# A hybrid attention block on one core: which preparation of weights is tied behind the last heads' work

## The chip, the core and the metric

The kernel runs on one core of a Trainium2 chip. The metric is the device time of one execution in microseconds. The core has five engines that matter here: TensorE (PE; its weight loads are listed apart as PEld), VectorE (DVE), ScalarE (ACT), GpSimd (POOL) and SyncE (SP, which only issues transfers). Each has a queue of its own and works through it in the order in which the program was built; engines meet only where one waits for another's semaphore.

## What is computed

A block of a decoder over 512 positions with 1024 channels, in float32. One normalised input is projected to queries, keys, values and a gate z for two branches of 8 heads each; one branch is attention with forget gates ("f"), the other block-sparse attention with rotary positions ("m"). Each branch's output is multiplied by silu(z), projected, weighted by a sigmoid gate, added, projected once more and added to the input.

```python
h = rms_norm(x, norm_g[layer])
fq, fk, fv, fz, mq, mk, mv, mz, ga, gb, fl = split_cols(h @ w_in[layer], IN_SPLITS)
...
y_fox = from_heads(fox_attention(q, k, v, log_f)) * jax.nn.silu(fz)
...
y_moba = from_heads(moba_attention(q, k, v)) * jax.nn.silu(mz)
merged = (jax.nn.sigmoid(ga + b_gate[layer, 0]) * (y_fox @ w_fox[layer])
          + jax.nn.sigmoid(gb + b_gate[layer, 1]) * (y_moba @ w_moba[layer]))
x = x + merged @ w_out[layer]
```

## The kernel before, in words

Every matrix product is made of three: each operand is split into a high half (rounded to the matmul's format) and a low half (what is left), and high x high, high x low and low x high are added in PSUM. For weights this split is the *preparation* of a chunk of 128 x 1024 elements: ScalarE writes the high half `wh_...` (`split`, L131, L134), VectorE subtracts it from the raw chunk and writes the low half `wl_...` (L136). Raw chunks come by transfers on SyncE's queue into four buffers `wr`; the high and the low halves have four buffers each (`wh`, `wl`). A raw buffer is free again when its low half has been written, a half's buffer when the last matmul has read it.

The work is written as a list of *units*, each a handful of matmuls with their eviction. `stream` (L192) appends the loads and preparations of a weight to two lists, `loads` and `preps`, in the order of L989: ..., mvb, wf0, wf1, wf2, wf3, GZ0, GA0, ... `pump(i)` (L179) traces what is due: preparations up to number i + 3, and a load as soon as the preparation that frees its buffer has been traced. `filler` (L1011) wraps each unit of a list so that `pump` is called just ahead of it; `ahead` (L1008) shifts the number by -2 for wf, by -1 for the first two units of a q, k or v weight.

Attention goes by four groups of four heads (`plan`, L1070). For each group `attn_group` (L509) returns pieces: Tr (transposes of a pair of heads, queries and keys to `QS`, `KH`, `KL`), Aa (scores `lg`, row maximum `negm` on VectorE, exponential `p` on ScalarE), Bb (transposes of `p` into `p_a`, `p_b`, `p_cc`, their split into `pth` on ScalarE and `ptl` on VectorE, the product `pv` with the values, and its eviction: `ysh` on ScalarE, then `yma` or `ymb` on VectorE; `pv` has one PSUM bank), Yp (a multiplication on GpSimd). Between the pieces `inter` (L1030) traces the group's units. Within the last heads (group "m", "b") these are the last two units of mvb and the eight units of wf0 to wf3: the projection of the f branch, 12 matmuls of 512 columns each (`unit_f`, L670: `pf`, L666 to L668, evicted by ScalarE into `f` at L680; `pf` has two banks). The order that is traced there is Aa(0), mvb, Yp of the group before, mvb, Aa(1), wf0, Tr(1), wf0, Bb(0), wf1, Aa(2), wf1, Bb(1), wf2, Yp(0), wf2, Aa(3), wf3, Bb(2), wf3, Bb(3).

Then the stage "gates" begins (L1103) with GZ0: the z gate of the m branch, computed by seven products of sums of blocks (`group`, L694), in the order 0, 2, 1, 3, 5, 4, 6. Product 0 uses the raw chunk mza as it is, product 2 the other chunk of mza; product 1 and later ones use differences with mzb that VectorE forms in place (L702). The matmuls are L741 (high x high), L743 (low x high) and L744 (high x low).

The program's order on each engine is made when the kernel is built: a planner goes through the traced instructions, takes what is ready first by its own estimate of the times, and among those the one traced first. Two things bind it: data, and a tie. `tc.issue_after(ins)` ties: what is traced in its block on the engine of `ins` is queued behind `ins` on that engine. It is an order in the queue and no wait. `last_on(engine)` (L1027) is the instruction traced last on an engine. In the kernel before, `filler` puts such a block on VectorE around `pump` for all units of wf:

```python
def go(i=first_prep[nm] + ahead(nm, n), u=u, late=nm[:2] == "wf"):
    if late:
        with tc.issue_after(last_on(mybir.EngineType.DVE)):
            pump(i)
    else:
        pump(i)
    u()
```

Of the kernel before, what the change touches and what calls it, by code (L numbers as in the profile page):

```python
# [29 lines left out]
def fox_moba_kernel(ctx: ExitStack, tc, xT, x, w_in, w_fl, w_fox, w_moba, w_out, cst, rope, out):  # L30
# [10 lines left out]
    stage = {}  # L41

    def enter(name):
        if stage:
            stage.pop("guard").__exit__(None, None, None)
        stage["guard"] = tc.tile_pool(name=name, bufs=1, reuse_waits="tile")
        stage["pool"] = stage["guard"].__enter__()
# [43 lines left out]
    def col(c, n=1):  # L91
        return cs[:, c:c + n]
# [3 lines left out]
    ones = con.tile([P, P], F32, name="ones")  # L96
    mask = con.tile([P, 512], F32, name="mask")
    enter("start")
    first_loads()
    wsc = t2("u", 3, "wsc", (P, 2))  # L100
# [75 lines left out]
    loads, preps, first_prep = [], [], {}  # L176
    done = {"loads": 0, "preps": 0}

    def pump(i):  # L179

        while True:
            j = done["loads"]
            if j < len(loads) and (j < WR or loads[j - WR][1] < done["preps"]):
                loads[j][0]()
                done["loads"] += 1
            elif done["preps"] < len(preps) and done["preps"] <= i + 3:
                preps[done["preps"]]()
                done["preps"] += 1
            else:
                return  # L190
# [65 lines left out]
    def make_sums(k):  # L256
        a, b = XT[k], XT[k + 4]
        out = []
        for o, x, y, op in ((b[:, HT:S], a[:, HT:S], b[:, HT:S], OP.add), (a[:, HT:S], a[:, 0:HT], a[:, HT:S], OP.subtract),
                            (a[:, 0:HT], b[:, HT:S], a[:, 0:HT], OP.subtract), (b[:, 0:HT], b[:, 0:HT], a[:, 0:HT], OP.subtract)):  # L260
            V.tensor_tensor(out=o, in0=x, in1=y, op=op)
        for i, f in enumerate((a, b)):
            hi = t2("sm", 2, "sum_h", dt=F32R)
            A.activation(hi, f, AF.Copy)
            V.tensor_tensor(out=f.bitcast(F32R), in0=f, in1=hi.bitcast(F32), op=OP.subtract)
            out.extend((d[2 * i:2 * i + 2, :, k, :].rearrange("s p t -> p s t"),
                        t.rearrange("p (s t) -> p s t", t=HT)) for d, t in zip(S_dram, (hi.bitcast(F32), f)))

        def store():
            for d, t in out:  # L270
                A.dma_start(out=d, in_=t)
        return store

    def load_sums():
        for i in (1, 0, 3, 2):
            SB[i] = [stage["pool"].tile([P, 4, HT], F32R, name=f"S{i}{hl}") for hl in "hl"]
            for d, t in zip(S_dram, SB[i]):
                nc.gpsimd.dma_start(out=t.bitcast(F32), in_=d[i])
# [65 lines left out]
    def rope_tables():  # L344
        nc.sync.dma_start(out=rp, in_=rope)
        for nm, c in (("mq", C_GQ), ("mk", C_GK)):
            tab = con.tile([P, NT, 32], F32, name=f"tab_{nm}")
            g = col(c, 16)
            G.tensor_tensor(out=tab[:, :, 0:16], in0=rp[:, :, 0:16],
                            in1=g[:, None, :].to_broadcast([P, NT, 16]), op=OP.mult)  # L350
            G.tensor_tensor(out=tab[:, :, 16:24], in0=rp[:, :, 16:24],
                            in1=g[:, None, 8:16].to_broadcast([P, NT, 8]), op=OP.mult)
            G.tensor_tensor(out=tab[:, :, 24:32], in0=rp[:, :, 24:32],
                            in1=g[:, None, 0:8].to_broadcast([P, NT, 8]), op=OP.mult)
            CA[nm] = tab
# [69 lines left out]
    def zero_kl():  # L425

        for o in range(2):
            Q2t[o] = stage["pool"].tile([P, S], F32R, name=f"Q2{o}")
        for b in range(2):
            for o in range(2):  # L430
                KLt.setdefault(o, []).append(stage["pool"].tile([P, S], F32R, name=f"KL{o}{b}"))
        for o in range(2):
            rows = slice(HD, P) if o == 0 else slice(0, HD)
            for tl in KLt[o] + [Q2t[o]]:
                G.memset(tl[rows, :].bitcast(F32), 0.0)
# [51 lines left out]
    def moba_begin():  # L487
        for o in range(2):
            rows = slice(HD, HD + 32) if o == 0 else slice(0, 32)
            for tl in KLt[o]:  # L490
                G.memset(tl[rows, :].bitcast(F32), 0.0)
# [503 lines left out]
    def units(name):  # L995
        k = name[:2]
        if k[0] == "G":
            return groups[name]
        if k == "wf":
            return [unit_f(int(name[2]), c) for c in range(2)]  # L1000
        if k == "wm":
            i = int(name[2])
            return [lambda c=c: merge_a(i, c) for c in range(2)]
        if k[1] == "z":
            return [unit_z(name, c) for c in range(2)]
        return [unit(name, t) for t in range(4)]

    def ahead(nm, n):  # L1008
        return n if nm[0] == "G" else -2 if nm[:2] == "wf" else -1 if nm[1] in "qkv" and n < 2 else 0

    def filler(names):  # L1011
        res = []
        for nm in names:
            nm, _, part = nm.partition(":")
            for n, u in enumerate(units(nm)):
                def go(i=first_prep[nm] + ahead(nm, n), u=u, late=nm[:2] == "wf"):
                    if late:
                        with tc.issue_after(last_on(mybir.EngineType.DVE)):
                            pump(i)
                    else:  # L1020
                        pump(i)
                    u()
                if not part or str(n) in part:
                    res.append(go)
        return res

    def last_on(engine):  # L1027
        return next(i for i in reversed(nc.cur_bb.bb.instructions) if i.engine == engine)

    def inter(a, b):  # L1030
        n, m = len(a), len(b)
        ia = ib = 0
        while ia < n or ib < m:
            if ib >= m or (ia < n and ia * m <= ib * n):
                a[ia]()
                ia += 1
            else:
                b[ib]()
                ib += 1

    def seq(names):
        for u in filler(names):
            u()
# [13 lines left out]
    forget_exp()  # L1057
    norm_row()
    pump(0)
    fz = filler(["fza", "fzb"])  # L1060
    for k, u in enumerate(fz):
# [3 lines left out]
    forget()  # L1065
    seq(["fva"])
    enter("attention")
    zero_kl()
    rope_tables()
    plan = (("f", "a", C_FQ, C_FK, ["fkb", "fqb", "fvb"]),  # L1070
# [5 lines left out]
    for n in range(4):  # L1076
        nxt = []

        def following(n=n, nxt=nxt):
            br, half, cq, ck = plan[n + 1][:4]  # L1080
            if n == 1:
                moba_begin()
            nxt.extend(attn_group(br, half, col(cq), col(ck)))
            nxt[0][0]()
        fill = filler(plan[n][4])
        if n < 2:
            for k, at in ((2 * n, 2), (2 * n + 1, 6)):
                store = []

                def with_sums(u=fill[at], k=k, store=store):  # L1090
                    u()
                    with tc.issue_after(last_on(mybir.EngineType.DVE)):
                        store.append(make_sums(k))

                def with_store(u=fill[at + 1], store=store):
                    u()
                    store[0]()
                fill[at], fill[at + 1] = with_sums, with_store
        inter(body + ([following] if n < 3 else []) + tail, fill)
        if n < 3:  # L1100
            body, tail = nxt[1][:1] + gate + nxt[1][1:], nxt[2]
            gate = nxt[3]
    enter("gates")  # L1103
    load_sums()
    for n, u in enumerate(filler(["GZ0"])):
# [135 lines left out]
```

## Time and profile before

| | |
|---|---|
| median of 3 runs | 424.71 us (424.6 to 425.9) |
| profiled execution | 424.55 us, span 422.8 us |
| TensorE matmul busy | 415.2 us, 98% of the span |
| TensorE weight loads busy | 387.7 us, 92% |
| VectorE busy | 334.5 us, 79% |
| ScalarE busy | 273.6 us, 65% |
| GpSimd busy | 109.5 us, 26% |
| granted TensorE clock | 0.998 of full speed |

The profile is of one execution; its time contains the span from the first to the last instruction and what lies around it. Busy shares are means over stages with different limits. The end of a matmul is modelled, so the timeline of TensorE is best read by its starts. In a timeline the columns are start and duration in us, engine, line, operation, the tile written and those read, partitions x elements, count; in brackets at the end the idle time of that engine just before and what ended it.

### The profile page before, as it was taken

What the parts mean: (1) busy time and instruction counts of PE and PEld (TensorE: products, weight loads), DVE (VectorE), ACT (ScalarE), POOL (GpSimd) and SP (SyncE); (2) the same over time, 40 slices, a digit from 0 to 9 for tenths busy, and PEclk for the clock granted to TensorE, in tenths of its full rate; (3) what the DMA queues carried; (4) which work ended last, traced back from release to release, by engine and by line L of the source; (5) the groups of instructions that cost most, each with busy time, mean ns of one, the idle gap of its engine ahead of it and who ended that gap; (6) DMA issues with size and microseconds to landing.
All of it is one profiled execution on the core that took longest, in us unless ns stands there. A gap on an engine that the chain in (4) does not pass through costs nothing.

```text
span 422.8 us, 7826 instructions
## 1 busy us (share of the span) xinstructions
PE 415.2 (98%) x2956; PEld 387.7 (92%) x2956; DVE 334.5 (79%) x571; ACT 273.6 (65%) x521; POOL 109.5 (26%) x127
## 2 busy tenths in 40 slices
PE   7999999999999999999999999999999999999996
PEld 6998899999999999999988789999999989988884
DVE  4669978798889877597457769998998675788982
ACT  4985337877788767797379845666756525685550
POOL 1059300252023880417501042134000020022240
PEclk9999999999999999999999999999999999999999
DMA  7981244654264432241211039705151726796494
GB/s 246 399 314 50 60 140 137 183 165 154 50 226 120 158 101 80 71 121 32 99 34 44 28 96 373 252 13 188 39 162 52 248 51 152 243 246 108 82 159 159
DMA packets 26373, 59.52 MB, mean 141 GB/s; under 512 B 3168, under 2 KB 7968, under 8 KB 26336
## 3 DMA queue, kind: packets, MB, share of 16 engines
q1 hardware_dynamic: 13552, 38.38, 27.5%
q0 software_dynamic: 3968, 9.44, 10.4%
q10 hardware_dynamic: 8816, 11.21, 9.1%
q8 instruction: 23, 0.38, 0.4%
q14 instruction: 14, 0.11, 0.1%
HBM read 48.37 MB, written 6.32 MB: 129 GB/s over the span
## 4 chain that ended last, share of the span: by engine, by line
PE 83%; DVE 6%; DMA 5%; ACT 2%; issue 2%; SPq 1%; DVEq 0%; ACTq 0%
PE pb_GB L744 3%; PE pb_GA L744 3%; PE pb_GA L741 3%; PE pb_GB L741 3%; PE pb_GA L743 3%; PE pb_GB L743 3%; PE po L943 3%; PE po L945 3%; PE po L944 3%; PE pv L609 2%; PE pv L610 2%; PE lg L556 2%; PE lg L555 2%; PE pf L666 2%; PE pf L668 2%; DMA x<-in_x_dram 2%
## 5 line engine op out<-in xcount | busy, mean ns | idle before, releaser
L330 POOL TENSOR_TENSOR ff<-ss,mh 128x8 f32<-128x8 f32 x16 | 28.3, 1771 | 59.4 <-DVE ss L328 58.8
L560 ACT ACTIVATE p<-p,negm 128x128 f32<-128x128 f32 (+1 forms) x64 | 35.6, 557 | 8.9 <-DVE negm L558 8.6
L558 DVE CUSTOM_DVE_ANT_0 p<-lg,mask 128x128 f32<-128x128 f32 (+1 forms) x64 | 30.2, 485 | 8.3 <-PE lg L556 6.9
L134 ACT ACTIVATE wh_GB<-wr_gb 128x1024 fp32r<-128x1024 f32 x14 | 14.6, 1058 | 13.9 <-PE pm L667 5.9
L905 ACT ACTIVATE wh_o<-wr_o 128x1024 fp32r<-128x1024 f32 x14 | 14.8, 1060 | 9.7 <-PE pb_GB L743 2.8
L555 PE MATMUL lg<-KH,QS 128*128 128x128 f32 (+1 forms) x64 | 20.9, 332 | 0.0
L136 DVE TENSOR_TENSOR wl_GB<-wr_gb,wh_GB 128x1024 fp32r<-128x1024 f32 x14 | 16.8, 1220 | 5.0 <-ACT wh_GB L134 5.0
L136 DVE TENSOR_TENSOR wl_GA<-wr_ga,wh_GA 128x1024 fp32r<-128x1024 f32 x14 | 19.2, 1388 | 1.5 <-ACT wh_GA L134 1.5
L906 DVE TENSOR_TENSOR wl_o<-wr_o,wh_o 128x1024 fp32r<-128x1024 f32 x14 | 16.9, 1220 | 2.4 <-ACT wh_o L905 2.3
L134 ACT ACTIVATE wh_GA<-wr_ga 128x1024 fp32r<-128x1024 f32 x14 | 14.4, 1056 | 6.9 <-DVE wr_ga L702 3.0
L826 POOL DMA_DIRECT2D uGB<-f x4 | 3.5, 871 | 58.2 <-issue 48.2
L529 DVE SCALAR_TENSOR_TENSOR QS<-p_qT,cs,QS 64x512 fp32r<-64x512 f32 x16 | 12.0, 750 | 5.7 <-ACT QS L528 5.4
L606 DVE TENSOR_TENSOR ptl<-p_b,pth 128x512 fp32r<-128x512 f32 x16 | 11.0, 684 | 6.2 <-ACT pth L605 6.1
L528 ACT ACTIVATE QS<-p_qT,cs 64x512 fp32r<-64x512 f32 x16 | 10.9, 681 | 4.4 <-PE p_qT L519 3.0
L744 PE MATMUL pb_GA<-Gh,wl_GA 128*128 128x256 f32 x48 | 13.5, 281 | 0.0
L744 PE MATMUL pb_GB<-Gh,wl_GB 128*128 128x256 f32 x48 | 13.5, 281 | 0.0
L743 PE MATMUL pb_GA<-Gl,wh_GA 128*128 128x256 f32 x48 | 13.5, 281 | 0.0
L741 PE MATMUL pb_GA<-Gh,wh_GA 128*128 128x256 f32 x48 | 13.5, 281 | 0.0
L741 PE MATMUL pb_GB<-Gh,wh_GB 128*128 128x256 f32 x48 | 13.5, 280 | 0.0
L743 PE MATMUL pb_GB<-Gl,wh_GB 128*128 128x256 f32 x48 | 13.5, 280 | 0.0
L666 PE MATMUL pf<-yhf,wh_wf 128*128 128x512 f32 x32 | 13.0, 407 | 0.3 <-ACT f L680 0.3
L668 PE MATMUL pf<-yhf,wl_wf 128*128 128x512 f32 x32 | 12.6, 403 | 0.2 <-DVE wl_wf L136 0.2
(483 smaller groups left out, 1821.4 us busy)
## 6 DMA issues: line engine op xcount, KB each, us to landing
wr_ga<-in_w_in_dram SPq DMA_DIRECT2D x8, 512.0 KB
wr_gb<-in_w_in_dram SPq DMA_DIRECT2D x8, 512.0 KB
wr_o<-in_w_out_dram SPq DMA_DIRECT2D x8, 512.0 KB
xt<-in_xT_dram SPq DMA_DIRECT2D x8, 256.0 KB
x<-in_x_dram SPq DMA_DIRECT2D x8, 256.0 KB
KH<-KH ACTq DMA_DIRECT2D x16, 128.0 KB
s_dramh<-sum_h ACTq DMA_DIRECT2D x8, 256.0 KB
s_draml<-xt ACTq DMA_DIRECT2D x8, 256.0 KB
```

The costliest lines, as they stand in the source:

```text
L134: A.activation(hi[:, :, 0:n], src, AF.Copy)
L136: eng.tensor_tensor(out=lo[:, q, 0:n], in0=src[:, q], in1=hi[:, q, 0:n].bitcast(F32), op=OP.subtract)
L330: G.tensor_tensor(out=f2, in0=ss.rearrange("p t h -> p (t h)"), in1=mh, op=OP.pow)
L555: T.matmul(lg[:, :n], qs[:, qt], kh[:, :n], start=True, stop=False)
L558: V.tensor_tensor_reduce(pt, lg[:, :n], mask[:, 512 - n:512], -0.125, 3.0e38, op0=OP.add, op1=OP.min, accum_out=mkn[:, hh, i:i + 1])
L560: A.activation(pt, pt, AF.Exp, bias=mkn[:, hh, i:i + 1], scale=-1.0, accum_out=rs[:, hh, i:i + 1])
L666: T.matmul(p, hi[:, k, cc], yh, start=(k == 0), stop=False)
L668: T.matmul(p, lo[:, k, cc], yh, start=False, stop=(k == 3))
L741: T.matmul(o, hi[:, k, cc], lh, start=(n < 3 and c == 0 and k == 0), stop=False, skip_group_check=True)
L743: T.matmul(o, hi[:, k, cc], ll, start=False, stop=False, skip_group_check=True)
L744: T.matmul(o, lo[:, k, cc], lh, start=False, stop=(k == 3), skip_group_check=True)
L906: V.tensor_tensor(out=wide(lo), in0=wide(R[key, c]), in1=wide(hi).bitcast(F32), op=OP.subtract)
```

## The change

The tie around `pump` for all wf units goes. In its place `pump` itself ties single preparations: those from z's first on (number `first_prep["GZ0"]` and above) that are traced while the heads are being traced, and those on two engines, behind the last VectorE and the last ScalarE instruction traced before them. A key "heads" in the dictionary `stage` says that the heads are being traced; `enter` therefore asks for the key "guard" instead of a dictionary that isn't empty.

```diff
     def enter(name):
-        if stage:
+        if "guard" in stage:
...
             elif done["preps"] < len(preps) and done["preps"] <= i + 3:
-                preps[done["preps"]]()
+                with ExitStack() as ties:
+                    if done["preps"] >= first_prep["GZ0"] and "heads" in stage:
+                        for engine in (mybir.EngineType.DVE, mybir.EngineType.Activation):
+                            ties.enter_context(tc.issue_after(last_on(engine)))
+                    preps[done["preps"]]()
                 done["preps"] += 1
...
-                def go(i=first_prep[nm] + ahead(nm, n), u=u, late=nm[:2] == "wf"):
-                    if late:
-                        with tc.issue_after(last_on(mybir.EngineType.DVE)):
-                            pump(i)
-                    else:
-                        pump(i)
+                def go(i=first_prep[nm] + ahead(nm, n), u=u):
+                    pump(i)
                     u()
...
     enter("attention")
+    stage["heads"] = True
...
+    stage.pop("heads")
     enter("gates")
```

## Rows read from the trace of the kernel before

**Rows 1.** Windows: window, its length, busy us (instructions) per engine, clock, DMA share, GB/s

```profile
core 0: us, PE busy (x) PEld busy (x) DVE busy (x) ACT busy (x) POOL busy (x), PEclk, DMA share, GB/s
210.00:220.00 10.00, 10.00 (x70) 9.29 (x70) 6.05 (x14) 7.57 (x15) 0.00 (x0) 1.00 0.13 29
220.00:230.00 10.00, 9.66 (x57) 8.08 (x56) 7.26 (x19) 8.49 (x21) 1.30 (x1) 1.00 0.15 40
230.00:240.00 10.00, 10.00 (x60) 8.33 (x59) 6.03 (x19) 8.76 (x23) 0.00 (x0) 1.00 0.10 26
240.00:250.00 10.00, 9.43 (x48) 7.36 (x48) 5.81 (x12) 6.00 (x17) 0.76 (x1) 1.00 0.21 68
250.00:260.00 10.00, 10.00 (x66) 8.93 (x65) 9.93 (x11) 4.45 (x7) 5.50 (x8) 1.00 0.86 272
300.00:320.00 20.00, 20.00 (x171) 20.00 (x170) 19.31 (x21) 12.96 (x19) 0.00 (x0) 1.00 0.34 107
```

**Rows 2.** Timeline of TensorE (PE) in the last heads

```profile
226.56 0.39 PE L555 MATMUL lg<-KH,QS 128*128 128x512 f32 x1
226.79 0.39 PE L556 MATMUL lg<-KL,QS 128*128 128x512 f32 x1
227.51 0.50 PE L666 MATMUL pf<-yhf,wh_wf 128*128 128x512 f32 x1 [0.34 <-ACT f L680]
...
233.67 0.60 PE L599 MATMUL p_b<-ident,p 128*128 128x128 f32 x4
234.02 0.48 PE L610 MATMUL pv<-ptl,v_mvb 128*128 128x512 f32 x1
...
240.01 0.63 PE L599 MATMUL p_a<-ident,p 128*128 128x128 f32 x4
240.99 0.50 PE L609 MATMUL pv<-pth,v_mvb 128*128 128x512 f32 x1 [0.35 <-DVE ymb L635]
...
241.56 0.34 PE L609 MATMUL pv<-pth,v_mvb 128*128 128x384 f32 x1
...
242.12 0.50 PE L668 MATMUL pf<-yhf,wl_wf 128*128 128x512 f32 x1 [0.22 <-DVE wl_wf L136]
...
249.97 0.60 PE L599 MATMUL p_a<-ident,p 128*128 128x128 f32 x4
250.47 0.50 PE L668 MATMUL pf<-yhf,wl_wf 128*128 128x512 f32 x1
...
256.12 0.37 PE L741 MATMUL pb_GZ<-Gh,wh_GZ 128*128 128x256 f32 x1
```

**Rows 3.** Timeline of VectorE (DVE) in the last heads

```profile
222.46 0.69 DVE L606 TENSOR_TENSOR ptl<-p_b,pth 128x512 fp32r<-128x512 f32 x1 [1.82 <-ACT pth L605]
...
240.25 0.68 DVE L635 TENSOR_TENSOR ymb<-pv,ysh 64x512 f32<-64x512 f32 x1
240.86 1.21 DVE L136 TENSOR_TENSOR wl_wf<-wr_wf,wh_wf 128x1024 fp32r<-128x1024 f32 x1
...
244.13 0.18 DVE L575 RECIPROCAL rinv<-rsum 128x8 f32<-128x8 f32 x1
248.47 0.70 DVE L635 TENSOR_TENSOR ymb<-pv,ysh 64x512 f32<-64x512 f32 x1 [4.16 <-ACT ysh L634]
249.20 1.23 DVE L136 TENSOR_TENSOR wl_wf<-wr_wf,wh_wf 128x1024 fp32r<-128x1024 f32 x1
250.34 2.31 DVE L136 TENSOR_TENSOR wl_GZ<-wr_mza,wh_GZ 128x1024 fp32r<-128x1024 f32 x1
```

**Rows 4.** Timeline of ScalarE (ACT) in the last heads

```profile
217.01 1.06 ACT L134 ACTIVATE wh_wf<-wr_wf 128x1024 fp32r<-128x1024 f32 x1
...
222.33 1.06 ACT L134 ACTIVATE wh_GZ<-wr_mza 128x1024 fp32r<-128x1024 f32 x1
...
226.86 0.60 ACT L680 ACTIVATE f<-pf 128x512 f32<-128x512 f32 x1
...
242.71 0.72 ACT L560 ACTIVATE p<-p,negm 128x512 f32<-128x512 f32 x1 [0.32 <-DVE negm L558]
```

**Rows 5.** Waits of SyncE's queue, 195 to 300 us: total, times, longest

```profile
SPq L707 <- DVE wl_wf L136: 61.3, 3, 39.6
```

## The prediction

> **What bounds the kernel now.** I first read the windows view over the stage in question [rows 1]. From 300 to 320 us TensorE is busy all the time and takes 171 matmuls of 256 columns in 20.00 us: that is how the back of the kernel looks, a TensorE that waits for nothing. In the last heads it is different: between 220 and 250 us TensorE shows 0.34 and 0.57 us of idle time, and VectorE and ScalarE, busy for 5.8 to 8.8 of 10 us, are not full either. So the bound there is the order of the queues, not an engine.
>
> Busy time hides part of it, because the end of a matmul is modelled. So the second view is TensorE's timeline [rows 2], read from start to start: undisturbed, 512 columns take 0.23 us to the next start (226.56 to 226.79), four transposes 0.35 (233.67 to 234.02), 384 columns some 0.17 (an estimate: three quarters of 0.23). What a start comes later than that is lost, and the first matmul behind a stall takes 0.50 instead of 0.39, another 0.10 (rounded down). There are four such places:
> - 226.79 to 227.51: 0.72 - 0.23 + 0.10 = 0.59, waiting for ScalarE's eviction f.
> - 240.01 to 240.99: 0.98 - 0.35 + 0.10 = 0.73, waiting for VectorE's ymb.
> - 241.56 to 242.12: 0.56 - 0.17 + 0.10 = 0.49, waiting for wl_wf.
> - 249.97 to 250.47: 0.50 - 0.35 + 0.10 = 0.25, where the row names no releaser, but the matmul reads the wl_wf that VectorE finished at 250.43 [rows 2, 3].
> The sum is 2.06 us, and the change can hardly give back more: behind these places TensorE's matmuls stand at full rate.
>
> The third and fourth views tell why [rows 3, 4]. VectorE issues the third and fourth low halves of wf at 240.86 and 249.20, each right behind ymb or with it just done (240.25; 248.47), which is the tie that the code draws. Yet their high halves were long there: the last ran on ScalarE at 217.01. And VectorE was idle meanwhile: 1.82 us ahead of 222.46, 4.16 us ahead of 248.47. On ScalarE z's first high half (wh_GZ) runs at 222.33, without a tie, 34 us before its first reader on TensorE at 256.12 [rows 2], and 4.5 us ahead of the eviction f at 226.86 for which TensorE then waits.
>
> **The change part by part.** The pump runs ahead of the units: mvb's units trace the preparation of wf0 and wf1, wf1's and wf2's units that of wf2 and wf3, wf3's that of z's first product. So the removed tie concerned three VectorE splits (wf2, wf3, z's first), and the new one concerns z's first alone, on both engines.
>
> 1. *wf2's and wf3's low halves lose their tie.* Two splits of 1.21 and 1.23 us [rows 3] can go as soon as their high halves are there, by 218.1 at the latest (217.01 + 1.06). Nothing is added or removed; they move ahead of head work by some 20 to 30 us. What they gain is the two waits: -0.49 and -0.25. What they cost is what they push back on VectorE: 2.44 us. Cover: between 210 and 220 VectorE is idle for 3.95 of 10 us [rows 1], and 1.82 us more before 222.46, and TensorE meanwhile has wf0's matmuls. I take the cost at nothing, since the idle time there (5.8 us at most) is over twice the work. If the cover fails, each split holds up the head's next small operation by up to 1.22, 2.44 in all; the other end is nothing.
>
> 2. *z's first high half gets a tie on ScalarE*, behind the last exponential traced, at 242.71 [rows 4]. It leaves 222.33 with its 1.06 us and comes at 243.4 at the earliest. ScalarE's queue between the two places moves up by at most 1.06; TensorE lost 0.59 to that queue. What stands between wh_GZ and f are head operations that wait for TensorE and VectorE themselves, so not all of it comes back: between 0 and -0.59, and I take the middle, -0.30. The second product's high half is traced behind the heads and has no tie, but takes the next of the same four wh buffers; I expect it behind the first, and count nothing for it.
>
> 3. *z's first low half keeps its place in the tracing order*, behind the reciprocal at 244.13, as before; today it ran at 250.34, since it stood behind wf3's split [rows 3]. After the change it may fill the 4.16 us in which VectorE waited for ScalarE's ysh. High half 243.4 to 244.5, low half to about 245.7: 10 us before 256.12. Cost nothing, the cover being those 10 us; were it gone, the price is the split itself, 1.22.
>
> 4. *SyncE's queue.* The loads of z's other two raw weights stand at its head and wait 61.3 us in all (three waits) for wl_wf, up to 39.6 us at once [rows 5]. With the splits early they go about 20 us earlier, 2 x 512 KB into a stretch in which the DMA engines are 0.10 to 0.15 busy [rows 1]; today they fall beside the loads of 250 to 260 (0.86). No TensorE row waits for them today: nothing. The heads' small transfers between 210 and 240 could meet them, which is one more way to part 1's price, not a further one.
>
> 5. *The wait at 240.99.* Its releaser is ymb, which the change does not touch; but wf2's matmuls no longer lack their low half and could stand in that hole. Between 0 and -0.73; I take 0, for the row that names the releaser.
>
> The sum: -0.49 - 0.25 - 0.30 = -1.04 us. The profiled execution took 424.55 us (span 422.8), 0.16 below the median of 424.71, so 423.51 for an execution like it and **423.7 us** for the median: 0.24% less. Whether this reaches the end: from 256 on TensorE is full, the preparation of z starts no later than before, and VectorE has 2.44 us less to do in the crowded 250 to 260 (9.93 of 10), so the later stages can move up as a whole.
>
> How much there is to win at all can also be read off the weight loads: PEld is idle 1.92 + 1.67 + 2.64 + 1.07 = 7.3 us between 220 and 260 [rows 1]. If all of that were waiting, the hole would be three times mine. The rows speak against it: a load takes 20.00 / 170 = 0.12 us in the full stretch, a matmul of 512 columns 0.23, so wf's matmuls leave the loader idle even undisturbed. The Trainium skill (Perfetto Trace Analysis, Identifying the Most-Contended Engine) says to judge TensorE's headroom by the busy share of LDWEIGHTS, not of matmuls; by that rule the change could win up to 7.3 us, by start-to-start 2.06.
>
> **The rivals.** What a measurement of this kernel can tell from no change is about 0.3%, 1.27 us: above 425.98 is slower, below 423.44 faster.
>
> *More comes back* (30%): with wf2 and wf3 free, the hole at 240 is filled too, and all of f's wait goes: -2.06, 422.65 us. For it: TensorE's order is planned with what is ready, and more is ready at every point. Against: an order fixed beforehand that met four holes will meet others.
>
> *It does not do what it says* (11%): the splits go early but TensorE's order stays, and the holes are waited out for pth, ymb or f instead; only the smallest, 0.25, goes: 424.46 us.
>
> *Slower* (16%): the untied splits get in front of head operations in VectorE's queue, which runs in order. Place: the chain score, maximum, exponential, pth, ptl of the last heads, where at 240.99 TensorE takes up ymb's result without any slack. Price: 2 x 1.22 in full, less what still comes back (0.74 + 0.30): +1.40, 426.1 us. It decides once a split stands closer than 1.22 us before an operation for which TensorE has no other work; against it speaks the idle time between 210 and 222.
>
> *The loader's whole idle time is waiting* (2%): 7.3 us come back, 417.4 us. The start-to-start readings speak against nearly all of it. The rule of the Trainium skill named above (Perfetto Trace Analysis) would allow this time at most.
>
> **How the numbers follow.** My forecast has the remaining 41%, of which some 4 points fall below 423.44 (f's wait gone in full gives 423.4). Faster: 30 + 2 + 4 = 0.36. Same: 37 + 11 = 0.48. Slower: 0.16. The range leaves out the slower case at its full price and the loader's, 18%; it reaches from 422.4 (422.65 and a quarter for the spread of the runs) to 425.8 (the median and most of one exposed split). The likeliest case alone: 423.4 to 424.4.
>
> **What would show it.** Right: wl_wf three and four before 225 on VectorE, no wait of TensorE for wl_wf, wh_GZ's first at 243 or later and no long run of ScalarE work from 222 to 227; wr_mzb loaded before 230; the first matmul of pb_GZ about 1 us earlier, and the same lead at 300 and at the end. Wrong: a new wait of TensorE for QS, negm, pth or ymb between 214 and 255 (slower), or pb_GZ's first matmul waiting for its weights; or a lead at 256 that is gone by 320, which would say that VectorE and not TensorE sets the pace there.

## The result and the profile after

The changed kernel takes 427.74 us (median of 8 runs, 427.05 to 428.2) against 425.22 us (424.6 to 427.0) before: a ratio of 1.0054 (95% interval 1.0038 to 1.007; intervals stand in square brackets from here on). That is 0.54% slower, above the 425.8 us at which the range ended. The profiled execution took 427.42 us with a span of 425.7 us, 2.9 us more than the 422.8 before.

Line numbers behind L188 are 4 higher than before (`pf` is L670 to L672, `ptl` L610, the products of GZ L745 to L748); the split keeps L134 and L136.

First the windows of the changed kernel; the first five rows answer to [rows 1].

```profile
core 0: us, PE busy (x) PEld busy (x) DVE busy (x) ACT busy (x) POOL busy (x), PEclk, DMA share, GB/s
220.00:230.00 10.00, 9.36 (x55) 7.71 (x54) 8.34 (x25) 8.01 (x22) 0.25 (x1) 1.00 0.31 98
230.00:240.00 10.00, 10.00 (x51) 8.34 (x51) 4.58 (x13) 5.87 (x16) 1.05 (x1) 1.00 0.08 16
240.00:250.00 10.00, 10.00 (x61) 8.82 (x60) 4.10 (x11) 6.83 (x17) 0.00 (x0) 1.00 0.08 25
250.00:260.00 10.00, 10.00 (x70) 9.19 (x69) 9.19 (x16) 7.02 (x15) 5.76 (x9) 1.00 0.57 208
260.00:270.00 10.00, 8.40 (x71) 8.20 (x70) 9.11 (x10) 6.63 (x8) 1.68 (x1) 1.00 0.76 274
270.00:280.00 10.00, 10.00 (x87) 10.00 (x86) 9.46 (x10) 5.38 (x8) 2.38 (x2) 1.00 0.51 177
280.00:290.00 10.00, 10.00 (x87) 10.00 (x86) 9.97 (x9) 6.08 (x8) 5.18 (x3) 1.00 0.14 46
290.00:300.00 10.00, 8.82 (x74) 8.61 (x74) 9.80 (x10) 6.24 (x8) 0.74 (x1) 1.00 0.48 166
```

The stage that was to gain has gained: TensorE shows no idle time from 230 to 260. The loss stands behind it, 1.60 us in 260 to 270 and 1.18 in 290 to 300, both stretches in which TensorE of the kernel before was full (10.00). VectorE does less than before in 230 to 250 (4.58 and 4.10 of 10 us for 6.03 and 5.81); from 250 to 300 it is over 9 of 10 busy in every stretch, as it was before (9.27 to 9.93).

TensorE's timeline, which answers to [rows 2], and below it the waits of TensorE from 195 to 320 us (total, times, longest):

```profile
227.59 0.39 PE L560 MATMUL lg<-KL,QS 128*128 128x512 f32 x1
228.56 0.50 PE L670 MATMUL pf<-yhf,wh_wf 128*128 128x512 f32 x1 [0.58 <-ACT f L684]
...
249.97 0.39 PE L560 MATMUL lg<-KL,QS 128*128 128x512 f32 x1
...
255.60 0.37 PE L745 MATMUL pb_GZ<-Gh,wh_GZ 128*128 128x256 f32 x1
...
265.80 0.28 PE L747 MATMUL pb_GZ<-S0l,wh_GZ 128*128 128x256 f32 x1
267.68 0.39 PE L748 MATMUL pb_GZ<-S0h,wl_GZ 128*128 128x256 f32 x1 [1.60 <-DVE wl_GZ L136]
...
290.41 0.28 PE L747 MATMUL pb_GA<-Gl,wh_GA 128*128 128x256 f32 x1
291.88 0.38 PE L748 MATMUL pb_GA<-Gh,wl_GA 128*128 128x256 f32 x1 [1.18 <-DVE wl_GA L136]
```

```profile
PE pb_GZ L748 <- DVE wl_GZ L136: 1.6, 1, 1.6
PE pb_GA L748 <- DVE wl_GA L136: 1.2, 1, 1.2
PE pf L670 <- ACT f L684: 0.6, 1, 0.6
```

No matmul waits for wl_wf or for ymb any more. Read from start to start as in the prediction, and summed over all starts from 220 to 260, TensorE lost 4.02 us before (1.19 + 0.85 + 1.63 + 0.35 by stretches of 10) and loses 2.96 now (1.72 + 0.22 + 0.62 + 0.40): 1.06 less. (The sums depend on what one takes as undisturbed for each shape, their difference hardly.) The first matmul of `pb_GZ` starts 0.52 earlier, at 255.60 for 256.12 [rows 2]; some 0.5 us had been lost before 195 us, where TensorE's matmuls stand in the same order in both kernels. Behind that the two new stalls cost about 1.82 and 1.46 us from start to start. 0.5 - 1.06 + 1.82 + 1.46 = 2.7 of the 2.9 us.

VectorE's timeline, which answers to [rows 3], with z's chain up to product 3 and the triple of low halves in front of the second stall:

```profile
215.42 1.23 DVE L136 TENSOR_TENSOR wl_wf<-wr_wf,wh_wf 128x1024 fp32r<-128x1024 f32 x1
...
219.04 1.23 DVE L136 TENSOR_TENSOR wl_wf<-wr_wf,wh_wf 128x1024 fp32r<-128x1024 f32 x1
...
252.93 0.20 DVE L579 RECIPROCAL rinv<-rsum 128x8 f32<-128x8 f32 x1
253.88 2.36 DVE L136 TENSOR_TENSOR wl_GZ<-wr_mza,wh_GZ 128x1024 fp32r<-128x1024 f32 x2 [0.74 <-ACT wh_GZ L134]
...
257.30 0.67 DVE L639 TENSOR_TENSOR ymb<-pv,ysh 64x512 f32<-64x512 f32 x1
257.90 0.67 DVE L610 TENSOR_TENSOR ptl<-p_a,pth 128x512 fp32r<-128x512 f32 x1
258.50 0.67 DVE L610 TENSOR_TENSOR ptl<-p_b,pth 128x512 fp32r<-128x512 f32 x1
259.09 1.21 DVE L706 TENSOR_TENSOR wr_mzb<-wr_mzb,wr_mzb 128x1024 f32<-128x1024 f32 x1
...
266.40 1.22 DVE L136 TENSOR_TENSOR wl_GZ<-wr_mzb,wh_GZ 128x1024 fp32r<-128x1024 f32 x1
...
286.13 5.69 DVE L136 TENSOR_TENSOR wl_GA<-wr_ga,wh_GA 128x1024 fp32r<-128x1024 f32 x3
```

The low half that ends the first stall (266.40 to 267.62) ran in the kernel before here:

```profile
262.83 1.22 DVE L136 TENSOR_TENSOR wl_GZ<-wr_mzb,wh_GZ 128x1024 fp32r<-128x1024 f32 x1
```

There it was done at 264.05, 2.5 us before it was wanted (266.56). It now comes 3.57 us later and is wanted 0.6 us earlier (265.92), so the slack is turned into a stall. Its chain begins with the pair at 253.88, for 250.34 [rows 3]: the same 3.5 us. From the pair to this low half VectorE takes 12.5 us in both kernels, with ptl and ymb of the last heads between z's instructions in both. The chain has not become longer; all of it starts later.

Why is z's pair late? ScalarE's timeline answers to [rows 4], SyncE's to [rows 5]:

```profile
252.08 0.72 ACT L564 ACTIVATE p<-p,negm 128x512 f32<-128x512 f32 x1
...
252.81 1.99 ACT L134 ACTIVATE wh_GZ<-wr_mza 128x1024 fp32r<-128x1024 f32 x2
```

```profile
216.67 3.95 SPq L711 DMA_DIRECT2D wr_mzb<-in_w_in_dram  x2
```

The tie does what it says: wh_GZ stands right behind the last exponential. But that exponential starts at 252.08, not at 242.71 [rows 4]. The last scores were computed at 249.97; in the kernel before the last of them is this:

```profile
239.65 0.40 PE L556 MATMUL lg<-KL,QS 128*128 128x512 f32 x1
```

What TensorE did in their place shows when the windows are taken for the matmuls of `pf` alone, here of the kernel before:

```profile
230.00:240.00 10.00, 5.04 (x19) 1.00 0.10 26
250.00:260.00 10.00, 4.94 (x20) 1.00 0.86 272
```

and of the changed kernel:

```profile
230.00:240.00 10.00, 8.04 (x33) 1.00 0.08 16
250.00:260.00 10.00, 3.04 (x12) 1.00 0.57 208
```

With both low halves there shortly after 220, wf2's matmuls are ready, and they are traced ahead of Aa(3). So 33 instead of 19 of wf's matmuls go in 230 to 240. Of all 96 of them, 84 instead of 52 start ahead of the last score: all of wf0 to wf2, and half of wf3's, which are traced behind Aa(3) and still go ahead of its last two scores. These go 10 us later, and 12 instead of 20 matmuls of wf are left beside the heads' tail.

**The theory** tested from here: freeing wf2 and wf3 lets TensorE spend wf's matmuls before the last scores; the heads' tail and all that is tied behind it slips by 9 us and meets z's chain on VectorE. **Its rivals**: the early splits hold VectorE's queue up (the rival of the prediction); the new ScalarE tie makes z late by itself; the place of the tie alone is wrong.

### The profile page after: what moved, and what is told of

Its sections match the earlier page's. It is cut to its first block, busy times and chain, and to the rows that moved or that the text cites. A ratio compares the mean times of both kernels' runs of the same rounds, so it can differ in the third digit from the quotient of the medians.

```text
span 425.7 us, 7828 instructions
## 1 busy us (share of the span) xinstructions
PE 415.5 (98%) x2956; PEld 388.4 (91%) x2956; DVE 336.0 (79%) x571; ACT 272.8 (64%) x521; POOL 108.3 (25%) x127
## 4 chain that ended last, share of the span: by engine, by line
PE 65%; DVE 16%; DMA 6%; ACT 5%; issue 4%; POOL 3%; SPq 1%; ACTq 0%; DVEq 0%; POOLq 0%
PE pb_GB L748 3%; PE pb_GB L747 3%; PE pb_GB L745 3%; PE po L947 3%; PE po L949 3%; PE po L948 3%; PE pb_GA L748 2%; PE pb_GA L747 2%; PE pb_GA L745 2%; DVE wl_GA L136 2%; DMA x<-in_x_dram 2%; PE pm L671 2%; PE pm L670 2%; PE pm L672 2%; PE lg L560 2%
## 5 line engine op out<-in xcount | busy, mean ns | idle before, releaser
L134 ACT ACTIVATE wh_GB<-wr_gb 128x1024 fp32r<-128x1024 f32 x14 | 14.6, 1058 | 13.9 <-PE pm L671 5.9
L136 DVE TENSOR_TENSOR wl_GA<-wr_ga,wh_GA 128x1024 fp32r<-128x1024 f32 x14 | 20.4, 1488 | 0.5 <-ACT wh_GA L134 0.5
L136 DVE TENSOR_TENSOR wl_GB<-wr_gb,wh_GB 128x1024 fp32r<-128x1024 f32 x14 | 16.8, 1220 | 4.9 <-ACT wh_GB L134 4.9
L134 ACT ACTIVATE wh_GA<-wr_ga 128x1024 fp32r<-128x1024 f32 x14 | 14.3, 1057 | 5.5 <-DMA wr_ga<-in_w_in_dram 4.2
L610 DVE TENSOR_TENSOR ptl<-p_a,pth 128x512 fp32r<-128x512 f32 x16 | 11.0, 685 | 5.6 <-ACT pth L609 5.3
L748 PE MATMUL pb_GA<-Gh,wl_GA 128*128 128x256 f32 x48 | 13.6, 283 | 1.2 <-DVE wl_GA L136 1.2
L670 PE MATMUL pf<-yhf,wh_wf 128*128 128x512 f32 x32 | 12.9, 404 | 0.6 <-ACT f L684 0.6
L748 PE MATMUL pb_GB<-Gh,wl_GB 128*128 128x256 f32 x48 | 13.5, 281 | 0.0
L745 PE MATMUL pb_GA<-Gh,wh_GA 128*128 128x256 f32 x48 | 13.5, 281 | 0.0
L745 PE MATMUL pb_GB<-Gh,wh_GB 128*128 128x256 f32 x48 | 13.5, 280 | 0.0
L610 DVE TENSOR_TENSOR ptl<-p_b,pth 128x512 fp32r<-128x512 f32 x16 | 10.9, 683 | 3.2 <-ACT pth L609 3.2
```

The costliest lines, as they stand in the source:

```text
L134: A.activation(hi[:, :, 0:n], src, AF.Copy)
L136: eng.tensor_tensor(out=lo[:, q, 0:n], in0=src[:, q], in1=hi[:, q, 0:n].bitcast(F32), op=OP.subtract)
L610: V.tensor_tensor(out=lo[:, :n], in0=p[:, :n], in1=hi[:, :n].bitcast(F32), op=OP.subtract)
L670: T.matmul(p, hi[:, k, cc], yh, start=(k == 0), stop=False)
L745: T.matmul(o, hi[:, k, cc], lh, start=(n < 3 and c == 0 and k == 0), stop=False, skip_group_check=True)
L748: T.matmul(o, lo[:, k, cc], lh, start=False, stop=(k == 3), skip_group_check=True)
```

## The experiments

Ratios are to the kernel before, measured beside it, with 95% intervals. Diffs are against the changed kernel where nothing else is said.

**One part alone.** First the tie of z on VectorE only, so that wf is free and z's high half on ScalarE is, too.

```diff
-                        for engine in (mybir.EngineType.DVE, mybir.EngineType.Activation):
+                        for engine in (mybir.EngineType.DVE,):
```

> wf's splits untied, z's first tied on VectorE alone (as in the kernel before), not on ScalarE. Theory (late z): the low half still waits for the last reciprocal near 252.9, so wl_GZ's wait of TensorE stays: ratio 1.003 to 1.006. Second theory (the ScalarE tie is the cost): the high half is back in the 220s and the loss is gone: ratio 0.998 to 1.001. Rival (queue of the heads): 1.005.

Measured: 426.09 us, 1.003 [1.0019, 1.0041]. wh_GZ runs at 222.91 again, the last exponential at 252.91, z's low halves at 253.88. TensorE's waits, 195 to 320 us:

```profile
PE pf L670 <- ACT f L684: 1.5, 1, 1.5
PE pb_GZ L748 <- DVE wl_GZ L136: 0.3, 1, 0.3
```

So freeing wf costs 0.30% without the new ScalarE tie, and the last exponential slips by 10 us with it. The place of the loss is another, though. With z's high half back ahead of f on ScalarE, TensorE waits 1.5 us for f (0.6 in the changed kernel); in z's stage it waits 0.3 us instead of 2.8, although z's low halves come at the same 253.88 as in the changed kernel. Next the reverse: wf2 and wf3 tied on VectorE as before, z tied on both engines.

```diff
-                    if done["preps"] >= first_prep["GZ0"] and "heads" in stage:
-                        for engine in (mybir.EngineType.DVE, mybir.EngineType.Activation):
+                    if done["preps"] >= first_prep["wf2"] and "heads" in stage:
+                        for engine in ((mybir.EngineType.DVE, mybir.EngineType.Activation,) if done["preps"] >= first_prep["GZ0"] else (mybir.EngineType.DVE,)):
```

> wf's splits tied on VectorE as before, z's first tied on both engines as in the change. Theory (late z): with wf tied the last exponential is back near 243, z's high half comes at about 243.5, its low half with wf's fourth near 250 as before, and nothing is late: ratio 0.998 to 1.001. Second theory (the ScalarE tie is the cost by itself): 1.003 or more, with a wait of TensorE for wl_GZ. Rival (queue of the heads): no loss, as no wf split is untied: 1.000.

Measured: 424.69 us, 0.9994 [0.9981, 1.0007]. The last exponential is at 244.99, wh_GZ right behind it at 245.71. A tied high half costs nothing as long as the place that it is tied to stays early. The second rival falls: the tie does nothing by itself. On top of a free wf it adds 0.24% (1.0054 to 1.003; the two intervals overlap a little). Then no tie at all:

```diff
-                        for engine in (mybir.EngineType.DVE, mybir.EngineType.Activation):
+                        for engine in ():
```

> No preparation is tied within the last heads, neither wf's nor z's. Theory (late z): the change lost because wf's matmuls, free of their wait, go ahead of the last head's scores, so that the last exponential (the place behind which z's first weights are tied) moves from 242.7 to 252.1, z's splits start 3.5 us later than before and TensorE waits for wl_GZ (1.8 us) and wl_GA (1.4 us). Without any tie z's first split runs in the 220s and both waits are gone: ratio to the kernel before 0.997 to 1.001, if the splits of z within the heads' queues cost less than the 1 us that the free wf gives. Rival (queue of the heads): the loss is the untied splits standing in front of the heads' small operations on VectorE; here more of them are untied, so the ratio is 1.005 or more.

Measured: 425.61 us, 1.0016 [1.0004, 1.0029], just above the expected upper end. The waits for wl_GZ and wl_GA are gone, although the last exponential is as late as ever (254.74); in their place TensorE waits 1.7 us (twice, 0.9 and 0.8) for negm, the last heads' row maximum: z's first split and first subtraction, at 225.41 and 228.30, now stand ahead of it in VectorE's queue. From 250 to 300 TensorE is never idle here. Late heads alone cost nothing behind 250; late heads with z tied behind them cost 0.54%.

**Which of the freed weights.** Only wf2's preparation is tied again; wf3's stays behind it by its buffer.

```diff
-                    if done["preps"] >= first_prep["GZ0"] and "heads" in stage:
-                        for engine in (mybir.EngineType.DVE, mybir.EngineType.Activation):
+                    if "heads" in stage and (done["preps"] >= first_prep["GZ0"] or done["preps"] == first_prep["wf2"]):
+                        for engine in (mybir.EngineType.DVE, mybir.EngineType.Activation)[:1 if done["preps"] < first_prep["GZ0"] else 2]:
```

> The changed kernel with the VectorE tie put back for wf2's split alone (wf3's low half takes the next of the same four buffers and so comes behind it). Theory (cover spent early): what loses is that wf2's matmuls, once free, go ahead of the last head's scores, so the heads end late and wf's matmuls are used up when z's splits and the tail of the heads meet on VectorE and ScalarE. With wf2 tied the scores come first again and 20 or more of wf's matmuls are left for the tail: ratio 0.995 to 1.001, no TensorE wait for wl_GZ, wl_GA, pth or ptl over 0.5 us. Rival (the missing tie of wf3 costs as much as that of wf2): 1.002 to 1.004.

Measured: 424.64 us, 0.9988 [0.9978, 0.9998]; last exponential 245.79, z's low halves 247.59, no wait in z's stage. And only wf3's (the same edit with `first_prep["wf3"]`):

> The changed kernel with the VectorE tie put back for wf3's split alone; wf2's is free. Theory (cover spent early): wf2's matmuls still go ahead of the last head's scores, the last exponential stays late (247 or later instead of 242.7), z's splits with it, and TensorE waits in the tail or for z's weights: ratio 1.002 to 1.006. Rival (the missing ties cost alike): about half of the change's loss, 1.002 to 1.004; rival (only wf3's matmuls matter as cover): 1.000 or less.

Measured: 425.15 us, 1.0001 [0.9987, 1.0014]: a miss. The last exponential is late, as expected (251.17), and z's pair is at 252.96, yet no matmul waits for z. Two rows of VectorE show how:

```profile
256.98 1.21 DVE L706 TENSOR_TENSOR wr_mzb<-wr_mzb,wr_mzb 128x1024 f32<-128x1024 f32 x1
...
263.19 1.22 DVE L136 TENSOR_TENSOR wl_GZ<-wr_mzb,wh_GZ 128x1024 fp32r<-128x1024 f32 x1
```

The pair is only 0.9 us ahead of the changed kernel's, the subtraction 2.1 (256.98 for 259.09), product 3's low half 3.2 (263.19 for 266.40). This order puts the subtraction ahead of the ptl, and 20 of wf's matmuls are left in 250 to 260 instead of 12. (Its wait of 0.8 us is for ymb, in 240 to 250.) Late heads are thus not enough for the loss: the order in which VectorE then takes tail and z, or the matmuls that are left, decides, too. This run does not tell the two apart.

**The tie's place alone.** wf free as in the change, but z tied behind the instructions that were traced last before wf2's first unit. (In this and the next two, `stage["heads"]` holds those two instructions.)

```diff
-                            ties.enter_context(tc.issue_after(last_on(engine)))
+                            ties.enter_context(tc.issue_after(stage["heads"][engine]))
...
-                def go(i=first_prep[nm] + ahead(nm, n), u=u):
+                def go(i=first_prep[nm] + ahead(nm, n), u=u, here=(nm, n) == ('wf2', 0)):
+                    if here:
+                        stage["heads"] = {e: last_on(e) for e in (mybir.EngineType.DVE, mybir.EngineType.Activation)}
                     pump(i)
```

> The changed kernel with one thing moved: z's first weights are tied on both engines behind the VectorE and ScalarE instructions that were traced last before wf2's first unit, not before wf3's. Theory (late z): the splits start some 3 us earlier than in the changed kernel (near 250) and the waits for wl_GZ and wl_GA shrink to under 0.5 us together, while the heads keep the 1 us that the free wf gives: ratio 0.997 to 1.001. Rival (queue of the heads): wf's splits stand where they stood, so the ratio stays 1.005.

Measured: 427.44 us, 1.0062 [1.0043, 1.0081]: a miss, as slow as the change. The waits for z are gone; two rows of TensorE and one of VectorE show what came instead.

```profile
260.36 0.50 PE L613 MATMUL pv<-pth,v_mvb 128*128 128x512 f32 x1 [0.98 <-ACT pth L609]
261.75 0.51 PE L614 MATMUL pv<-ptl,v_mvb 128*128 128x512 f32 x1 [0.88 <-DVE ptl L610]
```

```profile
252.16 2.95 DVE L136 TENSOR_TENSOR wl_GZ<-wr_mza,wh_GZ 128x1024 fp32r<-128x1024 f32 x2
```

Now z's pair stands ahead of the tail, and the tail is late: its products wait at 260 and 261, where no matmul of wf is left (the last is at 253.40). An earlier tie moves the collision; it doesn't take it away. The third rival falls, as far as one other place can tell.

**TensorE's order.** wf's splits stay free and z stays tied on both engines. wf2's and wf3's units are traced behind the last scores, and their matmuls queued behind these on TensorE. (The units of mvb, wf0 and wf1 are spread anew over the pieces ahead of the scores by this, so a little more than the order of wf2 and wf3 moves.)

```diff
-                            ties.enter_context(tc.issue_after(last_on(engine)))
+                            ties.enter_context(tc.issue_after(stage["heads"][engine]))
...
-        inter(body + ([following] if n < 3 else []) + tail, fill)
+        if n < 3:
+            inter(body + [following] + tail, fill)
+        else:
+            inter(body, fill[:6])
+            stage["heads"] = {e: last_on(e) for e in (mybir.EngineType.DVE, mybir.EngineType.Activation)}
+            pump(first_prep["wf3"] - 2)
+            held = last_on(mybir.EngineType.PE)
+
+            def behind_scores(u):
+                def go():
+                    with tc.issue_after(held):
+                        u()
+                return go
+            inter(tail, [behind_scores(u) for u in fill[6:]])
```

> wf's splits free and early as in the change, z's first tied on both engines behind the last head's exponentials as in the change; but wf2's and wf3's units are traced behind the last head's scores and their matmuls queued behind them on TensorE. This puts back the order of TensorE without putting back the tie of the splits. Theory (cover spent early): the scores come early again, 48 matmuls of wf are left as cover for z's splits and the tail, the waits for wl_GZ and wl_GA go; TensorE may lose up to 1 us before the scores, where nothing fills its holes: ratio 0.996 to 1.002. Rival (the free splits in VectorE's queue are the cost): 1.005, as they stand where the change has them.

Measured: 424.52 us (423.63 to 425.26), 0.9984 [0.9973, 0.9995]; by the two ratios 0.7% faster than the changed kernel, and 0.16% below the kernel before. The windows of `pf`, then a row of VectorE:

```profile
230.00:240.00 10.00, 5.42 (x23) 1.00 0.13 27
250.00:260.00 10.00, 4.83 (x20) 1.00 0.64 238
```

```profile
244.69 2.36 DVE L136 TENSOR_TENSOR wl_GZ<-wr_mza,wh_GZ 128x1024 fp32r<-128x1024 f32 x2 [0.75 <-ACT wh_GZ L134]
```

wf's splits are as early as in the change (216.26 and 219.89). So early splits on VectorE are not what costs the 0.54%; with the scores ahead of wf2's matmuls z's pair runs 9.2 us earlier, and of TensorE's waits from 195 to 320 only f's 0.6 remains. The first rival falls. One unit less held back, wf2's first left ahead (`fill[:7]` and `fill[7:]` in the same edit):

> As the kernel before it in this list, but wf2's first unit stays ahead of the last head's scores and fills the holes there; 36 matmuls are held behind the scores. Theory (cover spent early): 0.995 to 1.001, the best of these if filling the holes ahead of the scores is worth more than the 12 matmuls of cover. Rival (free splits in VectorE's queue): 1.005.

Measured: 426.36 us, 1.003 [1.0011, 1.0049]: a miss. 33 of wf's matmuls go in 230 to 240, as in the change. The last exponential is nearly early (245.50), z's pair, too (247.29), and nothing waits for z. But two products of the tail wait:

```profile
260.30 0.50 PE L613 MATMUL pv<-pth,v_mvb 128*128 128x512 f32 x1 [0.57 <-ACT pth L609]
261.54 0.51 PE L614 MATMUL pv<-ptl,v_mvb 128*128 128x512 f32 x1 [0.74 <-DVE ptl L610]
```

These two waits are 1.3 us in all, 0.3%. One unit of twelve matmuls is enough to bring the tail's collision back, here with a last exponential only 2.8 us later than in the kernel before.

Side by side: the matmuls of wf that the window 250 to 260 counts, the time for which the windows show TensorE idle on either side of 250 us (one profiled execution each), and the ratio.

| kernel | z's first tied on | wf in 250 to 260 | idle 220 to 250, us | idle 250 to 300, us | ratio |
|---|---|---|---|---|---|
| before | VectorE | 20 | 0.91 | 0 | 1 |
| wf tied, z on both | both | 21 | 0.72 | 0 | 0.9994 |
| wf2 tied | both | 20 | 0.73 | 0 | 0.9988 |
| wf3 tied | both | 20 | 1.29 | 0 | 1.0001 |
| four units held back | both | 20 | 0.64 | 0 | 0.9984 |
| three units held back | both | 15 | 0.74 | 1.31 | 1.003 |
| place of the tie moved | both | 12 | 0.65 | 1.92 | 1.0062 |
| changed | both | 12 | 0.64 | 2.78 | 1.0054 |
| z on VectorE only | VectorE | 12 | 1.54 | 0.33 | 1.003 |
| no tie | none | 14 | 1.82 | 0 | 1.0016 |

Four of the rows on which the third column rests, of wf3 tied, three units held back, z on VectorE only and no tie:

```profile
250.00:260.00 10.00, 4.94 (x20) 1.00 0.82 286
250.00:260.00 10.00, 3.73 (x15) 1.00 0.41 141
250.00:260.00 10.00, 3.02 (x12) 1.00 0.49 177
250.00:260.00 10.00, 3.37 (x14) 1.00 0.23 78
```

TensorE stalls for more than 1 us behind 250 only where two things meet: 15 or fewer of wf's matmuls are left there, and z's first weights are tied on ScalarE, too. With 20 left the same ties cost nothing; with 12 or 14 left and ScalarE's tie gone the idle time stands in front of 250, at f or at the row maximum. The table sorts the runs; what each stall waits for is read from its rows above.

**Is it VectorE's load in z's stage?** The changed kernel without the four subtractions that form z's differences. (It leaves that part of the computation out: all products of GZ use raw chunks. With the work a step of the chain goes, too, since a later high half waits for its difference; the run does not separate the two.)

```diff
         def sub(o, a, b):
-            V.tensor_tensor(out=o, in0=a, in1=b, op=OP.subtract)
+            if not gz:
+                V.tensor_tensor(out=o, in0=a, in1=b, op=OP.subtract)
```

> The changed kernel without the four subtractions that form z's weights (wr_mza and wr_mzb, 1.22 us each on VectorE, inside the chain from z's first split to its later ones); z's later products then use the raw chunks, so that part of the computation is left out. Theory (VectorE is full from 253 us on, since z's chain starts late): 4.9 us less in that chain remove TensorE's waits for wl_GZ (1.8) and wl_GA (1.4): ratio 0.996 to 0.999. Rival (the later weights wait for their transfers): the wait for wl_GA stays, 1.002 or more.

Measured: 424.88 us, 0.9996 [0.9982, 1.001], a hair above the expected range. Four instructions of 1.22 us less on VectorE, and both waits, for wl_GZ and for wl_GA 24 us later, are gone, with the heads as late as in the change (last exponential at 252.25). Then the opposite, z's first low half written twice, once in the changed kernel and once in the kernel before:

```diff
                 B[n] = split(R[key], CW, f"{name}{n}")
+                if gz and n == 0:
+                    V.tensor_tensor(out=B[n][1][:, :, 0:CW], in0=R[key], in1=B[n][0][:, :, 0:CW].bitcast(F32), op=OP.subtract)
```

> The changed kernel with z's first low half written twice (one more VectorE instruction of 1.22 us at the head of z's chain). Theory (VectorE is full from 253 us on): the whole of it is lost, ratio to the kernel before 1.0075 to 1.009 (1.0054 plus 1.22 us). Rival (the waits come from the order and VectorE has room): 1.004 to 1.007.

> The kernel before with the same instruction written twice. Theory: there z's chain starts 3.5 us earlier, so 1.22 us more fits, ratio 0.999 to 1.001. Rival (VectorE is the bound there too): 1.003.

Measured: 432.35 us, 1.0168 [1.0144, 1.0192], in the changed kernel; 425.85 us, 1.0017 [1.0004, 1.003], in the kernel before, just above its expected range and without a new wait of TensorE. The first is a miss: it lies far above the 1.0075 to 1.009 of the theory and above the rival, too. One instruction of 1.22 us costs some 0.7 us before the change and 4.8 us after it (1.0168 - 1.0054 = 0.0114 of 425). From 250 to 300 TensorE of the changed kernel is now idle for 5.2 us instead of 2.78, nearly all of it in waits for weights of GZ and GA, in four of the five stretches of 10 us; in the fifth VectorE is busy for only 7.18 us. So the place in the chain counts and not the load alone. The kernel before had part of a split to spare here, the changed one has none; that what is late is late again in every later product is read from these waits.

## Why the prediction was wrong

- **wf's splits** (part 1): at 215.42 and 219.04, both waits for wl_wf gone, as forecast: -0.74. "I take the cost at nothing" did not hold in full: f's wait is 0.97 - 0.23 + 0.10 = 0.84 for 0.59. TensorE's wait for f is 0.6 us in the changed kernel and in each run above that leaves both splits free and ties z on both engines; it is 0.3 in both runs that tie wf2. On VectorE the first row maximum behind the split at 219.04 starts at 220.30, for 218.36 before, and 0.5 us of that is the shift from ahead of 195.
- **z's high half** (part 2): at 252.81, so out of f's way; I counted -0.30. With wf tied as before, the same move leaves f's wait at 0.3 us, so it gained nothing there. With wf free it is worth more than I counted: with the high half back at 222.91, f's wait is 1.5 instead of 0.6.
- **The wait for ymb** (part 5): taken as 0, it is gone in full, -0.73. The four places together: -0.74 + 0.25 - 0.73 = -1.22; over all starts -1.06. The sum of -1.04 was right by luck: a gain taken as 0 (ymb) and a gain that came out as a loss (f) nearly offset each other.
- **SyncE's loads** (part 4): at 216.67, no matmul waits for them: right.
- **The step that failed** is part 3 and the sentence built on it. "High half 243.4 to 244.5, low half to about 245.7: 10 us before 256.12" took the place of the last exponential from the trace of before, while the change itself moves it by 9.4 us (252.08 for 242.71): the freed matmuls of wf go ahead of the last scores. "The preparation of z starts no later than before" was thus wrong by 3.5 us (253.88 for 250.34); the cover of 10 us was gone, and TensorE stalled for wl_GZ and wl_GA. "VectorE has 2.44 us less to do in the crowded 250 to 260" counted only what leaves: 9.93 fell to 9.19 there, while from 260 to 300 VectorE is busy for 38.3 of 40 us (before: 37.9). In 230 to 250 it is idle for 11.3 of 20 us (before: 8.2), while z's work, tied behind the last heads, waits. One of the signs named for being wrong came true: the lead at 256 is gone by 268.
- **The slower rival** (16%, 426.1 us) had the sign, not the mechanism: with the same early splits and another order on TensorE the kernel runs at 0.9984. The price was to be 2 x 1.22 less the gain, paid in the heads; measured there is the 0.25 us at f, and 1.82 + 1.46 us at two places some 10 and 35 us behind the first matmul of `pb_GZ`.
- **The loader's idle time**: from 220 to 260 it fell from 7.3 us to 2.29 + 1.66 + 1.18 + 0.81 = 5.9, by 1.4 where the starts gained 1.06; what is left of it is twice the 2.96 that the starts lose. From 260 to 300 it is 1.80 + 1.39 = 3.2 us, about the 3.28 that the starts lost. By the Trainium skill (Perfetto Trace Analysis, Identifying the Most-Contended Engine) the weight loads' busy share tells the headroom; this trace agrees in the stage of 256-column matmuls and not in that of 512-column ones.

What stays open: why each order of tail and z on VectorE lands where it does (wf3 tied at 1.0001, one unit held less at 1.003, both expected otherwise) is shown as a collision, not predicted by any rule; and the half microsecond before 195 us, where TensorE's order is the same, has no cause that a run shows.

## What to carry to other kernels

A wait that is taken away frees work, and here the freed work went first because it was traced first: ask what the engine will do in place of waiting, and what then comes later. A tie names an instruction, not a time; forecast where that instruction will be after the change. Work that can run at any time (wf's matmuls) is cover for a later tight place, and the next stage's slack on the second-busiest engine must be counted before it is spent.

## What the runs showed of the hardware

**VectorE beside GpSimd.** The second stall ends with a triple of low halves that takes 5.69 us instead of 3 x 1.22 = 3.66. GpSimd works meanwhile: its first multiplication runs from 286.36 to 288.50. The second and third low half, and GpSimd's second multiplication between them, in the changed kernel:

```profile
287.27 2.32 DVE L136 TENSOR_TENSOR wl_GA<-wr_ga,wh_GA 128x1024 fp32r<-128x1024 f32 x1
288.47 2.27 POOL L794 TENSOR_TENSOR ymb<-ymb,uGZ 128x512 f32<-128x512 f32 x1
289.51 2.31 DVE L136 TENSOR_TENSOR wl_GA<-wr_ga,wh_GA 128x1024 fp32r<-128x1024 f32 x1
```

The second low half ends at 289.59, 1.09 us after GpSimd's first multiplication; the third ends at 291.82, 1.08 after GpSimd's second (290.74). In the kernel before the same GpSimd work meets a VectorE that had part of its splits done: its splits take 1.22, 1.72 and 1.49 us, 0.77 more than undisturbed instead of 2.03, and the two long ones again end 1.08 or 1.09 us after a multiplication of GpSimd, whenever they started. So in these rows a low half does nearly all of its 1.22 us of work after the GpSimd instruction beside it has ended. The triple ends at 291.82, the stall at 291.88; without the 2.03 us the low half would have been there at about 289.9 (its high half is done at 288.64), before it was wanted at 290.5. That is read from the rows and was not tried. The Trainium skill (SBUF — State Buffer, SBUF: two separate sides) says that VectorE and GpSimd share a pair of ports, and that of a VectorE instruction with two SBUF inputs and a GpSimd instruction that reads SBUF the one that starts first gets the pair for the whole instruction, while the other is blocked; the ends of the low halves agree with that.

**The clock after stalls.** In the profiled execution of the changed kernel with the low half written twice, two windows:

```profile
260.00:270.00 10.00, 8.52 (x67) 8.02 (x66) 8.74 (x9) 5.34 (x7) 1.35 (x2) 1.00 0.66 238
270.00:280.00 10.00, 10.00 (x74) 10.00 (x74) 7.18 (x8) 4.10 (x6) 2.46 (x2) 0.83 0.64 211
```

Behind a stretch with 1.48 us of idle TensorE (and 0.91 in the ten before it) the granted clock is 0.83 in the mean, a part of the stretch at 1.2 instead of 2.4 GHz, and TensorE runs 74 matmuls without a gap where the changed kernel runs 87: an estimated 13 x 0.115 = 1.5 us. This execution took 433.02 us at a mean granted clock of 0.995. The other three of this kernel took 430.98, 432.58 and 432.11 us at 1.0, 0.999 and 0.999: they are nearly as slow without such a fall, so the clock is not the cause of the 4.8 us. The changed kernel, with 1.60 us of idle time in its own 260 to 270, keeps 1.00.
